# Two heads of an HGRN2 pair make their steps in one job instead of in turn

## The chip, the core and the metric

The kernel runs on one core of a Trainium2 chip. Its time is the device time of one execution in microseconds (us); of the kernel before, three runs gave a median of 1096.72 us (1095.92 to 1097.88). Engines go by the profile's names: PE is TensorE (its weight loads are PEld), DVE is VectorE, ACT is ScalarE, POOL is GpSimd, SP is the engine that issues most DMAs.

## What is computed

Two layers of an encoder over 512 tokens of 1024 channels. Each layer normalises x, multiplies it with one wide matrix, feeds four head groups A, B, C and D, gates each, and adds the product of all four with an output matrix to x. Group A, the part that changes, has four heads of 128 channels; each is a gated linear recurrence, run forwards and backwards over the sequence and added:

```python
def _hgrn2_scan(q, k, v, log_f):
    # S_t = diag(f_t) S_{t-1} + k_t v_t^T, o_t = S_t^T q_t, in chunks
    attn = jnp.einsum('bhtd,bhsd,bhtsd->bhts', qb, kb, decay)
    o = (jnp.einsum('bhts,bhsv->bhtv', attn, vb)
         + jnp.einsum('bhtd,bhdv->bhtv', qb * jnp.exp(b), S))
    ...
# per head: o = rmsnorm(o_forward + o_backward) * silu(z)
```

Group B is windowed attention, C a matrix-memory recurrence, D attention into 256 memory tokens.

## The kernel before

**Projections.** Nearly all of the time is PE work on the projections. Weights come in blocks of 512 KB (`load_w`, line 385); of each block ACT makes a rounded copy `wh` and DVE the rest `wl`, and PE adds three products per tile (`wh` with the high and the low part of the input, `wl` with the high part) into a PSUM tile `pj`. `mm` (line 257) and `gmm` (line 260) issue every product, so nearly all PE rows have L258 or L261; operations on DVE, ACT and POOL all go through one helper and have L152.

**An A head** (`mix_A`, line 550) is a generator that works between these products. It goes through seven levels, block length m = 1, 2, 4 to 64. A level's products are `per_block` (line 566): for m up to 16 sixteen products of 32 weight columns, for m = 32 again 32 columns, for m = 64 eight products of 64 columns, all into one PSUM tile `s`. Level 1 has in addition a first set of 32 products (the diagonal), into a second `s` tile that ACT copies out (line 579). Behind the products of a level DVE multiplies K2 (line 598) and then Q2 (line 601) with the decays of the level, and only then takes the level's products out of PSUM with a predicated copy (line 603, and 608 for m = 32). The pool `ps` (line 223) has two buffers for each name, so there are two `s` tiles at any time. After the levels come transposes of K2 (L635, tile `tr`), the states (`s`), the output (`o`), a root mean square on ACT and DVE (`rsqrt`, line 368, a chain of 12 small DVE operations), and at last the transposes of the normalised output (L669).

**What sets the order.** `Weave` (line 159) keeps the jobs beside the projections. Every group of projection products calls `tick` with its PE time; a job whose due time has come makes its next step there, and is due again after the PE time that it reports plus a latency that it names (`A_LAT0` for the start, `A_LAT` for a level, by pair, `A_LAT2` and `A_LATN` for the tail; in ns, line 73). `join` makes the rest of a job's steps at once. The four heads work as two pairs: pair 0 beside the projections of its own values and of group B, pair 1 beside those of C and D. In a pair the two heads are two jobs, the second set off by half an `A_LAT`, so that they alternate. What is so recorded is then sorted by a scheduler of the framework into one fixed order for each engine; an engine carries out its rows in this order.

Of the kernel before, what the change touches and what calls it, by code (L numbers as in the profile page):

```python
# [14 lines left out]
P = 128  # L15
# [54 lines left out]
              + [O_CK, O_CQ, O_CZ, O_CZ + 256, O_DQ, O_DQ + 256])  # L70
OUT_ORDER = ((0, 1), (2, 3))

A_LAT0, A_LAT, A_LAT2, A_LATN = 5500, (5400, 4600), 500, 27000
B_LATP, B_LAT = 300, 1150
AHEAD = 2
AHEAD_V = 1
# [82 lines left out]
class Weave:  # L159
# [10 lines left out]
    def mark(self, name):  # L170
        self.name = name
        self._mark(name)
# [34 lines left out]
def trunk(tc, a, dbg=None, mark=lambda s: None):  # L207
    wv = Weave(mark)
# [5 lines left out]
    with es:  # L214
# [17 lines left out]
        def u4(shape, dt=F32):  # L232
            return u4p.tile([P] + shape, dt, tag="u4", name=nm("u4"))
# [5 lines left out]
        def a2(shape, dt=F32):  # L239
            return a2p.tile([P] + shape, dt, tag="a2", name=nm("a2"))  # L240
# [144 lines left out]
        def load_w(n, *more):  # L385

            his, los = [], []
            for m in more:
                his.append(m[0])
                los.append(m[1])  # L390
            for _ in range(n - len(more)):
                raw = wp.tile([P, 4, 256], F32, tag="wr", bufs=3, name=nm("wr"))
                hi, lo = [wp.tile([P, 4, 272], F32R, tag=t, bufs=WB, name=nm(t)) for t in ("wh", "wl")]
                sy.dma_start(raw.rearrange("p k c -> p (k c)"), a["wpk"][nblk[0]])
                nblk[0] += 1
                with tc.high_priority() if nblk[0] > 4 else contextlib.nullcontext():
                    act.copy(hi[:, :, 0:256], raw)
                    dve.tensor_tensor(lo[:, :, 0:256], raw, hi[:, :, 0:256].bitcast(F32), ALU.subtract)
                his.append(hi)
                los.append(lo)  # L400
            if n == 1:
                return hi, lo
            return (lambda k: his[k // 4][:, k % 4]), (lambda k: los[k // 4][:, k % 4]), his, los
# [6 lines left out]
        def proj_tok(h, w, n, evac, nt=NC):  # L410

            whi, wlo = w[:2]
            nh = sum(t.ap[1][1] for t in h[0]) // 4
            pts = [pj() for _ in range(nt // 2)]
            for kh in range(nh):
                for c in range(nt):
                    o = pts[c // 2][:, (c % 2) * 256:(c % 2) * 256 + n]
                    for k in range(4 * kh, 4 * kh + 4):
                        hh = rows(h[0], k)[:, c * P:(c + 1) * P]
                        hl = rows(h[1], k)[:, c * P:(c + 1) * P]  # L420
                        last = k == 4 * nh - 1

                        gmm(o, hh, whi(k)[:, :n], k == 0 and c % 2 == 0, False)
                        gmm(o, hh, wlo(k)[:, :n], False, False)
                        gmm(o, hl, whi(k)[:, :n], False, last)
                        if k % 2 == 1:
                            wv.tick(6 * n / 2.4)
                    if kh == nh - 1 and c % 2 == 1:
                        with tc.high_priority():
                            evac(c - 1, pts[c // 2].rearrange("p (c n) -> p c n", c=2)[:, :, :n])  # L430
# [15 lines left out]
        def proj_ch(h, w, evacs, nt=T, bank=pj):  # L446

            whi, wlo = w[:2]
            pts = [bank() for _ in evacs]
            for kh in range(2):  # L450
                for b, pt in enumerate(pts):
                    for k in range(4 * kh, 4 * kh + 4):
                        wh = whi(k)[:, b * P:(b + 1) * P]
                        wl = wlo(k)[:, b * P:(b + 1) * P]
                        hh = rows(h[0], k)[:, 0:nt]
                        hl = rows(h[1], k)[:, 0:nt]
                        mm(pt[:, :nt], wh, hh, start=(k == 0), stop=False)
                        mm(pt[:, :nt], wh, hl, start=False, stop=False)
                        mm(pt[:, :nt], wl, hh, start=False, stop=(k == 7))
                        wv.tick(3 * nt / 2.4)  # L460
                    if kh == 1:
                        with tc.high_priority():
                            evacs[b](pt[:, :nt])
# [54 lines left out]
        def gate_proj(h, w):  # L518
            gz = u4([NC, 256])
            proj_tok(h, w, 256, lambda c0, pv: silu_gate(gz, c0, pv))  # L520
            return gz
# [154 lines left out]
        def group_A(l, h, pr, yT, between=None, before=None, raw=None):  # L676

            mark(f"projA{pr}")
            last_exp.clear()
            if raw is None:  # L680
                w = load_w(2)
                q = [a2([512]) for _ in range(2)]
                proj_ch(h, w, [lambda pv, t=t: act.copy(t, pv) for t in q])
            else:
                q, h0, R, jobR = raw
            F2 = K2 = v = gz = None
            jobs = []

            def ev(pv, b, d):

                with tc.issue_after(last_exp[0].ins) if last_exp else contextlib.nullcontext():
                    act.activation(F2[b][:, d], pv, AF.Sigmoid)
                    act.activation(K2[b][:, 1 - d], pv, AF.Sigmoid, scale=-1.0)
                if l > 0:
                    hd = pr * 2 + b
                    dve.tensor_scalar(F2[b][:, d], F2[b][:, d], oml[:, hd:hd + 1], lb[:, hd:hd + 1], ALU.mult, ALU.add)
                    dve.tensor_scalar(K2[b][:, 1 - d], K2[b][:, 1 - d], oml[:, hd:hd + 1], None, ALU.mult)

            def gates():
                nonlocal F2, K2  # L700
                F2 = [u4([2, 512]) for _ in range(2)]
                K2 = [u4([2, 512]) for _ in range(2)]
                for d in (1, 0):
                    w = load_w(2)
                    if raw is not None:
                        def scaled(pv, b, d):
                            wv.join(jobR)
                            t = a2([512])
                            dve.tensor_tensor(t, pv, R, ALU.mult)
                            ev(t, b, d)  # L710
                        proj_ch(h0, w, [lambda pv, b=b, d=d: scaled(pv, b, d) for b in range(2)], bank=psc if d else pj)
                    else:
                        proj_ch(h, w, [lambda pv, b=b, d=d: ev(pv, b, d) for b in range(2)])

            def values():
                nonlocal v, gz
                w = load_w(2)
                v = u4([NC, 256])
                proj_tok(h, w, 256, lambda c0, pv: act.copy(v[:, c0:c0 + 2], pv))
                if between is not None:  # L720
                    between()
                    mark(f"projA{pr}")
                w = load_w(2)
                gz = gate_proj(h, w)

            def go():
                for b in range(2):
                    jobs.append(wv.spawn(f"mixA{pr * 2 + b}", mix_A(l, pr * 2 + b, F2[b], K2[b], q[b],
                                         lambda c, b=b: v[:, c, b * P:(b + 1) * P],
                                         lambda c, b=b: gz[:, c, b * P:(b + 1) * P], yT), after=b * A_LAT[pr] / 2))  # L730
            if pr == 0:
                gates()
                wv.join(*jobN)
                jobN.clear()
                if raw is not None:
                    jobM.append(wv.spawn("memn", mem_norm(), after=M_LAT))
                go()
                values()
            else:
                values()  # L740
                before()
                mark(f"projA{pr}")
                gates()
                go()
            return jobs
# [454 lines left out]
        def mem_norm():  # L1200
            yield 0, 0
            spread(jobM.pop(0), Rm)
            yield 450, M_LAT2
            mem0.append(mem_kv(0))
            next(mem0[0])
            yield 0, 0
# [284 lines left out]
        for l in range(NL):  # L1491
# [19 lines left out]
            jobs = group_A(l, h, 0, yA, raw=raw)  # L1511
# [3 lines left out]
            b = group_B(l, h)  # L1515
# [10 lines left out]
            jobs = group_A(l, h, 1, yA, lambda: gates.append(next(grC)), lambda: wv.join(jobB, *gates))  # L1526
# [48 lines left out]
```

## Time and profile before

| | |
|---|---|
| median of 3 runs | 1096.72 us |
| profiled execution, its own time | 1095.96 us |
| its span | 1094.2 us |
| PE busy | 1070.1 us, 98% |
| DVE, ACT, POOL busy | 752.9, 545.3, 108.9 us |
| granted TensorE clock, mean | 0.998 of full speed |

The span is what the trace covers, some 1.8 us less than the execution's own time. A busy PE means that a product is under way, not that the array is full. In the rows a line gives the start, the time until the last of the merged instructions ends, engine, source line, operation, tile written and tiles read, shapes and how many instructions were merged; idle time ahead and what ended it stand in brackets. A float32 product that isn't of the rounded type is recorded as two instructions, so the 16 products of a level are 32 records.

### The profile page before, as it was taken

The page shows a single profiled execution, that of the slowest core. Times are in us where ns is not written, and L with a number is a line of the kernel's source. Part 1 is how long each engine was busy: PE and PEld are TensorE (multiplying, and loading weights), DVE is VectorE, ACT ScalarE, POOL GpSimd, SP SyncE. Part 2 cuts the span into 40 slices and gives each one's busy share as a digit, 9 for nine tenths or more (in the row PEclk, how much of TensorE's full clock was granted, in tenths as well). Part 3 has the DMA queues.
Part 4 walks back from the last instruction along what each step waited for, and adds up shares of the span by engine and source line. Part 5 has one row for each costly group of instructions (what it writes and reads, how often), then busy time and mean ns, then how long its engine had stood idle before and what let it go on. Part 6 is the DMA issues. An engine that isn't in the chain of part 4 may idle for free.

```text
span 1094.2 us, 22817 instructions
## 1 busy us (share of the span) xinstructions
PE 1070.1 (98%) x9148; PEld 962.3 (88%) x9148; DVE 752.9 (69%) x1819; ACT 545.3 (50%) x1152; POOL 108.9 (10%) x184
## 2 busy tenths in 40 slices
PE   8999999999999999999999999999999999999997
PEld 6899898998988897887798999889989789889997
DVE  5997547695676958867373776487858668687664
ACT  7645247666435444345473434376754354433544
POOL 0000001220000222011000000013100013020200
PEclk9999999999999999999999999999999999999999
DMA  9332242122223346222443221311122233272111
GB/s 346 104 111 79 74 139 99 40 79 61 81 85 81 106 104 191 74 75 96 152 156 114 79 80 59 95 63 59 61 77 80 78 89 100 95 216 82 59 40 78
DMA packets 36857, 107.62 MB, mean 98 GB/s; under 512 B 6208, under 2 KB 9920, under 8 KB 36752
## 3 DMA queue, kind: packets, MB, share of 16 engines
q1 hardware_dynamic: 36032, 103.67, 29.9%
q0 software_dynamic: 720, 2.50, 0.6%
q8 instruction: 72, 1.18, 0.4%
q14 instruction: 33, 0.27, 0.1%
HBM read 101.89 MB, written 4.26 MB: 97 GB/s over the span
## 4 chain that ended last, share of the span: by engine, by line
PE 78%; DVE 12%; ACT 4%; DMA 3%; issue 1%; POOL 0%; SPq 0%; ACTq 0%; DVEq 0%; POOLq 0%
PE pj L258 34%; PE pj L261 27%; DVE u L152 4%; PE s L258 4%; PE o L258 4%; DVE a L152 3%; PE s L261 3%; DVE wl L152 2%; PE o L261 2%; ACT u L152 1%; PE tr L862 1%; ACT a L152 1%; ACT wh L152 1%; DMA u<-in_memT 1%; DMA u<-in_xT 1%
## 5 line engine op out<-in xcount | busy, mean ns | idle before, releaser
L261 PE MATMUL pj<-wh,u 128*128 128x256 f32 x1984 | 386.7, 286 | 2.8 <-ACT u L152 1.2
L258 PE MATMUL pj<-u,wh 128*128 128x512 f32 (+1 forms) x1216 | 374.8, 389 | 2.5 <-ACT u L152 1.3
L261 PEld LDWEIGHTS pj<-wh,u 128*128 128x128 f32 x1984 | 314.2, 188 | 7.4 <-ACT u L152 1.6
L152 DVE TENSOR_TENSOR wl<-wr,wh 128x1024 fp32r<-128x1024 f32 (+1 forms) x162 | 194.4, 1201 | 123.1 <-ACT wh L152 122.0
L261 PE MATMUL pj<-wl,u 128*128 128x256 f32 x992 | 278.5, 281 | 0.0
L258 PEld LDWEIGHTS pj<-u,wh 128*128 128x128 f32 x1216 | 216.8, 188 | 44.1 <-ACT u L152 2.1
L152 ACT CAST wh<-wr 128x1024 fp32r<-128x1024 f32 (+1 forms) x162 | 164.3, 1015 | 153.5 <-PE pj L258 72.2
L258 PE MATMUL pj<-u,wl 128*128 128x512 f32 (+1 forms) x608 | 232.6, 383 | 0.0
L261 PEld LDWEIGHTS pj<-wl,u 128*128 128x128 f32 x992 | 187.1, 189 | 0.3
L258 PEld LDWEIGHTS pj<-u,wl 128*128 128x128 f32 x608 | 114.2, 188 | 23.0
L152 DVE TENSOR_TENSOR u<-u,a 128x512 f32<-128x512 f32 (+1 forms) x104 | 74.1, 730 | 19.5 <-PE s L261 16.4
L258 PE MATMUL pj<-wh,u 128*128 128x256 f32 (+1 forms) x320 | 62.8, 287 | 0.0
L152 POOL TENSOR_SCALAR u<-u,rB 128x256 f32<-128x256 f32 (+1 forms) x64 | 35.5, 567 | 245.7 <-DVE rB L152 132.1
L258 PEld LDWEIGHTS o<-u,u 128*128 128x128 f32 x384 | 48.2, 191 | 4.5 <-issue 2.5
L258 PE MATMUL o<-u,u 128*128 128x129 f32 (+1 forms) x384 | 50.2, 275 | 1.9 <-DVE dnC L152 1.9
L258 PEld LDWEIGHTS pj<-wh,u 128*128 128x128 f32 x320 | 51.0, 188 | 0.7 <-issue 0.5
L152 POOL TENSOR_TENSOR u<-u,cf 128x512 f32<-128x512 f32 x16 | 22.6, 1412 | 234.4 <-DMA u<-rdr 129.1
L258 PE MATMUL pj<-wl,u 128*128 128x256 f32 (+1 forms) x160 | 45.3, 283 | 0.0
L152 DVE TENSOR_TENSOR u<-u,u 128x512 f32<-128x512 f32 (+2 forms) x48 | 38.7, 838 | 5.7 <-ACT a L152 4.5
L258 PE MATMUL s<-u,a 128*128 128x256 f32 (+1 forms) x224 | 40.6, 301 | 0.0
L152 ACT ACTIVATE u<-u,nmB 128x256 f32<-128x256 f32 (+1 forms) x64 | 35.8, 561 | 8.7 <-DVE nmB L152 6.5
L152 ACT COPY u<-u 128x512 f32<-128x512 f32 x40 | 26.8, 686 | 26.4 <-DVE u L152 13.0
(222 smaller groups left out, 1379.5 us busy)
## 6 DMA issues: line engine op xcount, KB each, us to landing
wr<-in_wpk SPq DMA_DIRECT2D x154, 512.0 KB, 3.5
u<-in_xT SPq DMA_DIRECT2D x16, 256.0 KB, 6.2
u<-rdr SPq DMA_DIRECT2D x16, 256.0 KB, 4.7
u<-gdr SPq DMA_DIRECT2D x16, 192.0 KB, 6.2
u<-in_x SPq DMA_DIRECT2D x4, 512.0 KB
u<-in_memT SPq DMA_DIRECT2D x4, 512.0 KB
xd<-u POOLq DMA_DIRECT2D x4, 512.0 KB, 5.0
u<-xd SPq DMA_DIRECT2D x4, 512.0 KB
```

Source lines behind the costliest of these rows:

```text
L152: r = f(*args, **kw)
L258: nc.tensor.matmul(out, l, r, start=start, stop=stop)
L261: nc.tensor.matmul(out, l, r, start=start, stop=stop, skip_group_check=True)
L862: nc.tensor.transpose(pt[:, j * P:(j + 1) * P], pr[e][:, j * P:(j + 1) * P], ident)
```

## The change

`go` no longer spawns two jobs. It makes both generators, and one job steps them in lock-step: each step of the job issues the step of the first head and then that of the second, reports the sum of their PE times and the longer of their latencies. The latencies in line 73 are longer.

```diff
-A_LAT0, A_LAT, A_LAT2, A_LATN = 5500, (5400, 4600), 500, 27000
+A_LAT0, A_LAT, A_LAT2, A_LATN = 6500, (6600, 5800), 2500, 25000
...
             def go():
-                for b in range(2):
-                    jobs.append(wv.spawn(f"mixA{pr * 2 + b}", mix_A(l, pr * 2 + b, F2[b], K2[b], q[b],
-                                         lambda c, b=b: v[:, c, b * P:(b + 1) * P],
-                                         lambda c, b=b: gz[:, c, b * P:(b + 1) * P], yT), after=b * A_LAT[pr] / 2))
+
+                heads = [mix_A(l, pr * 2 + b, F2[b], K2[b], q[b], lambda c, b=b: v[:, c, b * P:(b + 1) * P],
+                               lambda c, b=b: gz[:, c, b * P:(b + 1) * P], yT) for b in range(2)]
+
+                def both():
+                    for s0, s1 in zip(*heads):
+                        yield s0[0] + s1[0], max(s0[1], s1[1])
+                jobs.append(wv.spawn(f"mixA{pr}", both()))
```

The number of products, copies and DMAs is the same. Outside the four stretches in which a pair works the order of PE stays, but for one set of group C's state products in each layer that moves by some products.

PE at the first level of pair 1 in layer 0. `s_3651` and `s_3686` are the diagonal and the level's products of the first head (`s_3639` and `s_3674` before), `s_3708` and `s_3743` those of the second; `pj` are projection products.

```order
 L261 MATMUL pj_3567<-wh_3561,u_20_113 128x256
+L261 MATMUL s_3651<-a_262_2056,u_548_3420 32x32 x32
+L261 MATMUL s_3686<-u_575_3575,u_576_3577 32x32 x16
 L261 MATMUL s_3708<-a_263_2057,u_549_3421 32x32 x32
-L261 MATMUL s_3743<-u_578_3598,u_579_3600 32x32 x16
 L261 MATMUL pj_3568<-wh_3561,u_15_108 128x256
 L261 MATMUL pj_3568<-wl_3562,u_15_108 128x256
+L261 MATMUL s_3743<-u_578_3580,u_579_3582 32x32 x16
```

The first head's two sets, which stood 12 projection products ahead of the second's, now stand right before them, and the second head's level stands two projection products behind. The other three pairs have the same four rows with the same two products between.

PE at the next level of the same pair: the first head's products (`s_3842`) and the second's (`s_3864`), which had 12 projection products between them.

```order
 L261 MATMUL pj_3805<-wl_3793,u_14_107 128x256
 L261 MATMUL pj_3805<-wh_3792,u_18_111 128x256
+L261 MATMUL s_3842<-u_575_3575,u_546_3418 32x32 x16
+L261 MATMUL s_3864<-u_578_3580,u_547_3419 32x32 x16
 L261 MATMUL pj_3805<-wh_3792,u_13_106 128x256
 L261 MATMUL pj_3805<-wl_3793,u_13_106 128x256
```

The two stand together, with some 60 projection products to the pair before and behind them.

PE at the end of the same pair: the transposes of the first head's output (`tr_4406`) and of the second's (`tr_4415`) among products of 512 columns.

```order
 L258 MATMUL pj_4443<-u_14_107,wl_4424 128x512
-L669 MATMUL tr_4415<-cf,u_547_3419 128x128
+L669 MATMUL tr_4406<-cf,u_546_3418 128x128
 L258 MATMUL pj_4442<-u_15_108,wh_4429 128x512
-L669 MATMUL tr_4415<-cf,u_547_3419 128x128
+L669 MATMUL tr_4406<-cf,u_546_3418 128x128
 L258 MATMUL pj_4442<-u_19_112,wh_4429 128x512
```

Where the second head's transposes stood, the first head's now stand; ahead of them come nine products of the second head's output and seven projection products since the last product of the first head's output. The second head's transposes follow some 24 projection products later.

## Rows read from the trace of the kernel before

**Rows 1.** The page: busy time, and granted clock in tenths by slices.
```profile
PE 1070.1 (98%) x9148; PEld 962.3 (88%) x9148; DVE 752.9 (69%) x1819; ACT 545.3 (50%) x1152; POOL 108.9 (10%) x184
...
PEclk9999999999999999999999999999999999999999
```

**Rows 2.** PE's waits, longest in total first: us in total, times, longest.
```profile
PE o L258 <- DVE dnC L152: 1.9, 2, 1.1
```

**Rows 3.** Windows, two pair stretches: PE, PEld, DVE, ACT, POOL, clock, DMA, GB/s.
```profile
50.00:107.00 57.00, 56.52 (x937) 53.78 (x936) 49.07 (x126) 27.83 (x47) 0.90 (x1) 1.00 0.29 94
286.00:353.00 67.00, 66.88 (x908) 57.30 (x908) 46.91 (x108) 27.99 (x59) 1.29 (x1) 1.00 0.25 75
```

**Rows 4.** PE's timeline around one head's level-4 products.
```profile
306.76 0.41 PE L261 MATMUL pj<-wh,u 128*128 128x256 f32 x2
...
308.19 0.28 PE L261 MATMUL pj<-wh,u 128*128 128x256 f32 x1
308.40 0.46 PE L261 MATMUL s<-u,u 128*32 128x32 f32 x32
308.79 0.38 PE L261 MATMUL pj<-wh,u 128*128 128x256 f32 x1
309.01 0.28 PE L261 MATMUL pj<-wl,u 128*128 128x256 f32 x1
```

**Rows 5.** PE's timeline, first level of pair 1, layer 0, both heads.
```profile
288.51 0.76 PE L261 MATMUL s<-a,u 128*32 128x32 f32 x58
...
289.17 0.54 PE L261 MATMUL s<-u,u 128*32 128x32 f32 x28
289.64 0.39 PE L261 MATMUL pj<-wh,u 128*128 128x256 f32 x1
289.86 0.28 PE L261 MATMUL pj<-wl,u 128*128 128x256 f32 x1
...
291.25 0.82 PE L261 MATMUL s<-a,u 128*32 128x32 f32 x63
...
291.91 0.54 PE L261 MATMUL s<-u,u 128*32 128x32 f32 x31
```

**Rows 6.** ACT's and DVE's timeline, the same place.
```profile
289.40 0.27 ACT L152 COPY a<-s 128x128 f32<-128x128 f32 x1 [1.15 <-PE s L261]
...
288.29 1.23 DVE L152 TENSOR_TENSOR wl<-wr,wh 128x1024 fp32r<-128x1024 f32 x1 [3.53 <-ACT wh L152]
289.43 2.10 DVE L152 TENSOR_TENSOR u<-u,u 128x512 f32<-128x512 f32 x2
291.37 0.32 DVE L152 COPY_PREDICATED a<-cu,s 128x128 f32<-128x128 uint8 x1
```

**Rows 7.** DVE's, then PE's timeline, first level of pair 1, layer 1.
```profile
830.52 0.30 DVE L152 COPY_PREDICATED a<-cu,s 128x128 f32<-128x128 uint8 x1
...
831.05 0.54 PE L261 MATMUL s<-u,u 128*32 128x32 f32 x32
```

**Rows 8.** Output to transposes, pair 1, layer 0: PE, ACT, DVE timelines.
```profile
337.00 2.39 PE L258 MATMUL o<-u,u 128*128 128x128 f32 x20
...
342.42 2.17 PE L258 MATMUL o<-u,u 128*128 128x128 f32 x18
...
350.67 0.39 PE L258 MATMUL pj<-u,wl 128*128 128x512 f32 x1
351.17 0.30 PE L669 MATMUL tr<-cf,u 128*128 128x128 f32 x1
...
339.43 0.28 ACT L152 ACTIVATE u<-o 128x128 f32<-128x128 f32 x1 [2.39 <-PE o L258]
...
340.61 0.17 DVE L152 TENSOR_SCALAR rq_v<-ssA 128x4 f32<-128x4 f32 x1 [3.59 <-ACT u L152]
...
348.50 0.16 DVE L152 TENSOR_SCALAR rq_y<-rq_v 128x4 int32<-128x4 int32 x1
...
350.68 1.13 DVE L152 SCALAR_TENSOR_TENSOR u<-o,rq_y,u 128x128 f32<-128x128 f32 x4
```

**Rows 9.** PE's timeline, a level-16 step of pair 0 in layer 0.
```profile
81.11 0.46 PE L261 MATMUL s<-u,u 128*32 128x32 f32 x32 [0.48 <-DVE rr L152]
```

## The prediction

> **What bounds the kernel now.** I read the page first. PE is busy for 98% of the span, at full clock in every slice [rows 1]: the kernel is as long as PE's queue. The list of PE's waits comes next. Its longest entry is 1.9 us in two waits [rows 2], so little can be won by ending waits, and what PE gains must come from the way its instructions follow each other. The table of stretches confirms it where the change works: while a pair of A heads is under way PE is busy for 56.52 of 57 us and 66.88 of 67 us, at clock 1.00 [rows 3]; the pairs of layer 1 look the same. DVE is busy for 49.07 of 57 us in the first stretch. Then I read PE's timeline at single steps, where a reader can see what inserting a head's step costs.
>
> **Fewer switches on PE.** Look at one head's step among projection products [rows 4]. Twelve products of 256 columns start between 306.76 and 308.19, 0.119 us apart. Around the step, the last one starts at 308.19, the head's 32 records at 308.40, the next projection product at 308.79 and the one after it not before 309.01: 0.82 us for two spacings of 0.119 and the step, which thus costs 0.58. The records themselves take 0.27 of it (0.46 until the last ends, less 0.2 for one record, and one spacing); the rest, 0.31, is paid once for a run of 32-column products, whatever its length. Where two heads' records follow each other, the second costs only its records. In the one place where that is already seen, the 63 diagonal records that run ahead of 31 more, records start 0.66/64 = 0.0103 us apart [rows 5], so 32 more would cost 0.33, and the switch saved would be 0.25. A saved switch is thus worth 0.25 to 0.31; I take 0.29, nearer to the undisturbed step. Runs of 64 columns were not priced apart and are taken alike.
>
> The number of runs follows from PE's order. Before, the four pairs make 57 separate runs of narrow products, and group C's states 4. After, the pairs make 38 (some levels still stand apart, since the scheduler puts a few projection products between the heads), C's states 6. So 61 - 44 = 17 switches go: 17 x 0.29 = **-4.9 us** (4.3 to 5.3). The products of 128 columns in the tail (transposes, states, outputs) I cost at nothing; if each merged tail set saved or lost one projection spacing of 0.12, twelve sets would move 1.4 us, which the range holds.
>
> **A wait that comes in.** Level 1 uses two PSUM tiles for each head, and there are only two `s` buffers. The second head's level-1 products need the buffer that the first head's level-1 products filled, and DVE empties that one only behind the two multiplications. Take the start of the first head's diagonal as zero, 288.51. ACT's copy of the diagonal ends at 289.67, 1.16 later; DVE's multiplications start at 289.43, and the predicated copy ends at 291.69, 3.18 after the start [rows 6]. The other three pairs show 3.2 as well. The weight cast ahead of the multiplications ends as the diagonal does, so it isn't what holds them. How soon PE follows is to be seen in layer 1, where the second head came just too early: copy ended at 830.82, PE started at 831.05 [rows 7], 0.23 later. So the second head's level can start 3.4 after zero. Where would PE be? The first head's sets take 0.99 (the last record starts at 289.17 + 0.54 - 0.21), the second diagonal 0.66, then 0.14 to a projection product, 0.22 to the next and 0.21 back [rows 4, 5]: 2.2 after zero. PE stands still for the difference, 3.4 - 2.2 = 1.2, less some 0.05 that the switch back may overlap: 1.15 in each of four pairs, **+4.6 us**. From below: if PE follows a copy within 0.1, 1.0 each, 4.0; from above: the second diagonal needs ACT's copy, 1.16 and 0.23 after zero, 0.4 past where it would start, and if nothing of that is swallowed by the later wait, 1.4 each, 5.6. Queued behind the waiting products on PE are projection products. DVE and ACT wait for those to take them out of PSUM, but have idle time of their own, and PE has nothing else to do: all of the wait is lost.
>
> The Trainium skill speaks against this change in the same place: "TensorEngine Tiling (Array Packing)", section PSUM Bottleneck, says that tiling speeds up the products but not the emptying of PSUM, which may become the bound. Here the 32-column records take 0.27 us and the emptying 3.2, which agrees; with the rule alone the sum would be the +4.6, with the switches alone -4.9.
>
> **Later levels** need no such wait: the buffer that a level needs was emptied in the level before, some 7 us of products earlier, and DVE's work for both heads of a level is four operations of 0.6 us and two copies. What it hides behind are some 60 projection products. **The tail of pair 1** is tighter than before, since the join leaves little to put between. From the last product of the first head's output to its transposes DVE and ACT need: squares, 339.43 to 340.61, 1.2; the root, 348.50 to 350.68 plus one step, 2.4; the first quarter of the output 0.35; and 0.15 to PE: 4.1. PE has 18 records of the other head, 2.0, and seven products of 512 columns, 1.6 [rows 8]: a wait of 0.45 in two layers, +0.9. The second head's transposes waited 0.27 before (351.17 against 350.67 and 0.23) and now come 7.6 us behind their output: -0.55 for two. Together **+0.35** (-0.5 to 1.5, had the root again to share DVE with other work). **One wait goes**: a level-16 step of pair 0 idled 0.48 us [rows 9]; its successors stand farther apart: **-0.5** (0 to -0.5).
>
> **Sum.** -4.9 + 4.6 + 0.35 - 0.5 = -0.45 us. The profiled execution took 1095.96 us, so 1095.5; the median of the runs is 0.76 above that execution, so **1096.3 us** in its terms. The bounds together give -5.3 + 4.0 - 0.5 - 0.5 = -2.3 and -4.3 + 5.6 + 1.5 = +2.8, or 1094.4 to 1099.5.
>
> **Rivals.** (1) *The wait doesn't bite.* If PE's wait at level 1 is mostly covered, for example because DVE starts its multiplications before the diagonal has ended, only the switches count: 1096.7 - 4.9 + 0.35 - 0.5 = 1091.7 us. For it: the predicated copy itself takes only 0.32. Against it: the multiplications overwrite what the diagonal reads, and the two stand ahead of the copy in DVE's queue [rows 6]. The skill's same page, section Key Properties, says that a change of tiling mode drains the engine; by that rule alone one arrives here. 15%. (2) *DVE becomes the bound, slower.* Both heads' multiplications now stand in a block on DVE, four times 0.6 and two copies of 0.2, 2.8 us, and a weight cast (1.23) that falls behind it is late for PE. Place: pair 0 of layer 0, where DVE is busy for 86% [rows 3]. If six levels each make PE wait 1 us there, 1096.3 + 6 = 1102 us. It decides once a cast ends less than about 2.8 us ahead of its first product. Against it: PE's waits name no cast, and DVE idled 3.53 ahead of one in pair 1 [rows 6]. 12%. (3) *The merge is less than it says*: no, the runs are counted in the order.
>
> **Chances.** A run of this kernel can tell about 0.2%, 2.2 us, from no change. Forecast 73%; it spreads with its bounds mostly within 2.2 us (62 of the 73), 7 below, 4 above. With the rivals: faster 7 + 15 = 22%, same 62%, slower 4 + 12 = 16%. The range goes from 1093.0, part of the way to rival 1, to 1099.5.
>
> **What would show it.** In the profile after: four waits of PE at `s` for DVE, each about 1.1 us, some 2 us after a pair's first diagonal; level steps with 64 records in one run, 0.55 us long; a wait of half a microsecond at the first transposes of pair 1's output; no projection product that waits for a cast. Four waits of well under 1 us, or records spaced wider in the merged runs, would prove the sum wrong on one or the other side.

## The result and the profile after

| | before | after |
|---|---|---|
| median of the runs made together | 1096.80 us (5 runs, 1095.92 to 1098.38) | 1102.07 us (5 runs, 1101.84 to 1105.05) |
| ratio, 95% interval | | 1.0051 (1.0040 to 1.0062) |
| profiled execution, its span | 1094.2 us | 1100.4 us |

The change made the kernel 0.5% slower, where 1096.3 us (1093.0 to 1099.5) was predicted. The page of the kernel after answers to [rows 1], and its list of PE's waits to [rows 2] (engine, tile, line, what it waited for: us in total, times, longest).

```profile
PE 1070.7 (97%) x9148; PEld 963.1 (88%) x9148; DVE 756.3 (69%) x1819; ACT 545.6 (50%) x1152; POOL 110.2 (10%) x184
```

```profile
PE tr L669 <- DVE u L152: 4.3, 4, 1.7
PE s L261 <- DVE a L152: 3.1, 4, 0.8
PE s L261 <- DVE u L152: 2.0, 2, 1.0
...
PE o L258 <- DVE dnC L152: 0.8, 1, 0.8
```

PE is busy for as long as before, and the kernel is 6 us longer: PE waits. The second entry is the predicted one, four times at level 1. The first is new and larger: 4.3 us at the transposes of the heads' output. The two windows of [rows 3] don't hold the same work now, but show the new idle time:

```profile
50.00:107.00 57.00, 56.10 (x918) 54.26 (x918) 45.57 (x119) 25.02 (x39) 0.61 (x1) 1.00 0.29 95
286.00:353.00 67.00, 65.68 (x908) 56.92 (x906) 43.04 (x92) 26.40 (x57) 0.14 (x1) 1.00 0.24 77
```

**Merged levels.** PE's timeline at a level of pair 1, as in [rows 4]: both heads' products stand in one run of 64 records.

```profile
301.42 0.28 PE L261 MATMUL pj<-wh,u 128*128 128x256 f32 x1
301.63 0.78 PE L261 MATMUL s<-u,u 128*32 128x32 f32 x64
302.34 0.38 PE L261 MATMUL pj<-wh,u 128*128 128x256 f32 x1
302.56 0.28 PE L261 MATMUL pj<-wl,u 128*128 128x256 f32 x1
```

From 301.42 to 302.56 is 1.14 us; without two spacings of 0.119 the run cost 0.90. Two separate runs of 0.58 [rows 4] cost 1.16, so a merge saves 0.26.

**Level 1.** PE, then ACT and DVE, first level of pair 1, layer 0 [rows 5, 6].

```profile
290.83 0.76 PE L261 MATMUL s<-a,u 128*32 128x32 f32 x58
...
291.49 0.54 PE L261 MATMUL s<-u,u 128*32 128x32 f32 x28
292.04 0.86 PE L261 MATMUL s<-a,u 128*32 128x32 f32 x64
292.83 0.39 PE L261 MATMUL pj<-wh,u 128*128 128x256 f32 x1
293.06 0.28 PE L261 MATMUL pj<-wl,u 128*128 128x256 f32 x1
294.11 0.54 PE L261 MATMUL s<-u,u 128*32 128x32 f32 x32 [0.78 <-DVE a L152]
```

```profile
291.73 0.27 ACT L152 COPY a<-s 128x128 f32<-128x128 f32 x1 [0.19 <-PE s L261]
...
291.73 2.10 DVE L152 TENSOR_TENSOR u<-u,u 128x512 f32<-128x512 f32 x2 [1.31 <-PE s L261]
293.67 0.29 DVE L152 COPY_PREDICATED a<-cu,s 128x128 f32<-128x128 uint8 x1
```

The second head's products start at 294.11, 3.28 behind the first diagonal, where 3.4 was predicted, and 0.15 behind the end of DVE's copy (293.96), where I took 0.23 [rows 7]. From the projection product at 293.06 to them is 1.05 us where an undisturbed switch takes 0.21: the wait costs 0.84. The second diagonal starts late as well: the last product ahead of it started at 291.82 (291.49 and 0.54, less 0.21 for one record), and it comes at 292.04, as soon as ACT has copied the first (292.00). Together that is 1.05 us in a pair, 4.2 in four.

**Tail of pair 1, layer 0.** PE first [rows 8], then DVE, then POOL.

```profile
345.90 4.18 PE L258 MATMUL o<-u,u 128*128 128x128 f32 x36
...
352.17 0.30 PE L669 MATMUL tr<-cf,u 128*128 128x128 f32 x1 [0.46 <-DVE u L152]
...
357.49 0.62 PE L258 MATMUL pj<-u,wh 128*128 128x512 f32 x2
359.75 0.30 PE L669 MATMUL tr<-cf,u 128*128 128x128 f32 x1 [1.64 <-DVE u L152]
```

```profile
352.71 0.16 DVE L152 TENSOR_SCALAR rq_v<-ssA 128x4 f32<-128x4 f32 x1
352.78 1.22 DVE L152 TENSOR_TENSOR wl<-wr,wh 128x1024 fp32r<-128x1024 f32 x1
353.92 1.26 DVE L152 TENSOR_SCALAR rq_y<-rq_v 128x4 int32<-128x4 int32 x1
355.09 0.74 DVE L152 SCALAR_TENSOR_TENSOR u<-tr,par,u 128x512 fp32r<-128x512 f32 x1
...
357.12 1.15 DVE L152 TENSOR_TENSOR rq_t<-rq_y 128x4 f32<-128x4 f32 x1
...
358.59 0.75 DVE L152 SCALAR_TENSOR_TENSOR a<-a,par,a 128x512 f32<-128x512 f32 x1
359.25 1.12 DVE L152 SCALAR_TENSOR_TENSOR u<-o,rq_y,u 128x128 f32<-128x128 f32 x4
```

```profile
352.86 2.29 POOL L152 TENSOR_TENSOR u<-u,cf 128x512 f32<-128x512 f32 x1 [91.69 <-DMA u<-rdr]
356.93 1.32 POOL L152 TENSOR_TENSOR u<-u,cf 128x512 f32<-128x512 f32 x1 [1.77 <-DMA u<-rdr]
```

The second head's output ends at 350.08, but DVE begins its root at 352.71, behind the first head's root and output. Into this chain fall a weight cast, two long steps of other jobs, and two steps of 128x4 that last 1.26 and 1.15 us instead of 0.16. Both lie under POOL's two mask additions for group C. PE comes at 357.95 (357.49 and two spacings of 0.23), and waits until 359.75. Layer 1 shows the same picture: waits of 0.47 and 1.75 us, and two 128x4 steps of 1.29 and 1.24 us.

```profile
901.78 0.30 PE L669 MATMUL tr<-cf,u 128*128 128x128 f32 x1 [1.75 <-DVE u L152]
```

In before the second root had ended at 350.7, just ahead of POOL's additions. POOL, then DVE, layer 0 of before:

```profile
351.68 1.29 POOL L152 TENSOR_TENSOR u<-u,cf 128x512 f32<-128x512 f32 x1 [91.39 <-DMA u<-rdr]
351.94 2.11 DVE L152 TENSOR_TENSOR wl<-wr,wh 128x1024 fp32r<-128x1024 f32 x1
```

There POOL came first, and it was DVE's weight cast that took 2.11 us instead of 1.22.

**Where the time went.** For each kernel I took the start of the same PE product ahead of and behind a stretch. The table gives what the stretch takes more than in before, in us, from one profiled run of each kernel (the start counts from the span's start); the columns behind "after" are experiments told below.

| stretch (before's time) | after | longer latencies | old latencies | early pair 1 | split |
|---|---|---|---|---|---|
| start, to 39.9 | +1.5 | +1.2 | +1.0 | +0.6 | +0.9 |
| pair 0, layer 0, 39.9 to 162.7 | -0.8 | -1.0 | +0.1 | -0.4 | -2.2 |
| pair 1, layer 0, 286.6 to 367.6 | +2.3 | +2.8 | +1.7 | +0.3 | -0.6 |
| C's states, 379.0 to 385.8 | +0.7 | +0.8 | 0.0 | 0.0 | 0.0 |
| C's last products, 416.5 to 441.7 | -0.7 | -0.1 | +1.4 | +1.4 | +1.4 |
| pair 0, layer 1, 613.2 to 729.5 | +0.8 | +0.7 | +1.0 | +1.1 | -0.7 |
| pair 1, layer 1, 825.7 to 905.9 | +2.0 | +2.1 | +1.4 | -0.9 | -1.8 |
| C's states, 918.4 to 925.2 | +0.7 | +0.8 | 0.0 | 0.0 | 0.0 |
| whole span | +6.2 | +7.6 | +6.2 | +1.5 | -3.4 |

The start holds the same instructions in the same order everywhere; its difference is none of the change's, and the last section returns to it and to the row of C's last products. Pair 1 is the place: +4.3 us in two layers.

### The profile page after: what moved, and what is told of

Read it like the earlier page. It is cut to its first block, busy times and chain, and to the rows that moved or that the text cites. A ratio compares the mean times of both kernels' runs of the same rounds, so it can differ in the third digit from the quotient of the medians.

```text
span 1100.4 us, 22823 instructions
## 1 busy us (share of the span) xinstructions
PE 1070.7 (97%) x9148; PEld 963.1 (88%) x9148; DVE 756.3 (69%) x1819; ACT 545.6 (50%) x1152; POOL 110.2 (10%) x184
## 4 chain that ended last, share of the span: by engine, by line
PE 77%; DVE 12%; ACT 5%; issue 2%; DMA 2%; POOL 1%; SPq 0%; ACTq 0%; POOLq 0%; DVEq 0%
PE pj L258 33%; PE pj L261 27%; PE o L258 5%; PE s L258 5%; DVE u L152 4%; DVE a L152 3%; PE s L261 2%; DVE wl L152 2%; ACT u L152 2%; ACT a L152 2%; ACT wh L152 1%; PE o L261 1%; PE tr L866 1%; DMA u<-rdr 1%; DVE rq_t L152 1%
## 5 line engine op out<-in xcount | busy, mean ns | idle before, releaser
L261 PE MATMUL pj<-wh,u 128*128 128x256 f32 x1984 | 379.8, 285 | 2.4 <-ACT u L152 1.2
L152 ACT ACTIVATE u<-o,dnC 128x128 f32<-128x128 f32 x32 | 11.7, 367 | 55.3 <-DVE dnC L152 54.0
```

What stands on the lines that cost most here:

```text
L152: r = f(*args, **kw)
L261: nc.tensor.matmul(out, l, r, start=start, stop=stop, skip_group_check=True)
```

## The experiments

My theory after the result had three parts: the wait at level 1; lateness (the longer latencies, and steps that report both heads' PE time, move pair 1's tail up against the join, where DVE has other work and is held by POOL); and merges that do save what they should. The rivals: lock-step itself puts one root behind the other; DVE is what bounds; switches cost nothing.

**1. Longer latencies alone**, heads alternating as before.

```diff
-A_LAT0, A_LAT, A_LAT2, A_LATN = 5500, (5400, 4600), 500, 27000
+A_LAT0, A_LAT, A_LAT2, A_LATN = 6500, (6600, 5800), 2500, 25000
```

> The kernel before with the four longer latencies alone; the two heads of a pair still alternate in two jobs. Lateness theory (the longer latencies move pair 1's tail up against the join, where DVE also has a weight cast to make and is held by POOL, so that PE waits for both heads' output there): PE waits about 0.6 us at the first head's output transposes and 1.5 to 2 us at the second's in each layer, none of the switches is saved and the level-1 bank wait does not come: 1096.8 + 4 = about 1101 us. Rival (it is the lock-step itself that puts the second head's root behind the first head's on DVE): no wait above 0.5 us at these transposes, 1096 to 1098 us.

1104.08 us against 1097.08 of before, ratio 1.0067 (1.0052 to 1.0082): at least as slow as the whole change, and 3 us above what I expected, which left out C's states (1.6 us in two layers) and the start (1.2). PE's timeline in the tails of pair 1, layer 0 and layer 1:

```profile
349.61 0.30 PE L669 MATMUL tr<-cf,u 128*128 128x128 f32 x1 [0.46 <-DVE u L152]
...
354.63 0.30 PE L669 MATMUL tr<-cf,u 128*128 128x128 f32 x1 [0.68 <-DVE u L152]
356.90 0.59 PE L669 MATMUL tr<-cf,u 128*128 128x128 f32 x2 [0.57 <-DVE u L152]
...
898.49 0.30 PE L669 MATMUL tr<-cf,u 128*128 128x128 f32 x1 [1.82 <-DVE u L152]
```

The waits at the transposes come without any lock-step, and C's states lose 0.8 us in each layer, as in after (0.7). Lock-step isn't needed for either; lateness is enough.

**2. Lock-step alone**, with the latencies of before.

```diff
-A_LAT0, A_LAT, A_LAT2, A_LATN = 6500, (6600, 5800), 2500, 25000
+A_LAT0, A_LAT, A_LAT2, A_LATN = 5500, (5400, 4600), 500, 27000
```

> The changed kernel (lock-step) with the four latencies of before. Lateness theory: the four waits at level 1 stay (4 x 1.07); pair 1's output products come 11 rows of PE (some 2.5 us) earlier than in the changed kernel, but still behind those of before, so PE still waits at the output transposes, 0.3 to 0.6 us for the first head and 0.5 to 1.5 us for the second, and C's states stay split: 1099 to 1101 us. Rival (the longer latencies alone did the harm, and lock-step with the old ones gives what was hoped): no wait at these transposes, 1096 to 1097.5 us.

1103.19 us, ratio 1.0053 (1.0040 to 1.0066), 2 us over the expected range; of the time over before, 1.4 us stand in C's last products and 1.0 in the start (last section). The first head's transposes waited 0.45 us in layer 0, the second's 0.65 and 0.53, and in layer 1 1.58. C's states did not split, against what I expected: that belongs to the longer latencies alone. So the old latencies don't help. With both heads' PE time in each step, pair 1 is late all the same: its output begins at 343.04, where before had the first head's at 337.00 [rows 8] and after both at 345.90.

**3. POOL's two additions left out.** This kernel leaves out the masks of group C's first head in each layer, and with them a part of the computation.

```diff
-                        gp.tensor_tensor(own, own, V(mge ...
+                        if hd > 0:
+                          gp.tensor_tensor(own, own, V(mge ...
```

> The changed kernel; POOL's two mask additions for the first head of group C are left out in each layer (part of the computation is missing). Theory (in pair 1's tail two of these POOL instructions hold DVE for 1.1 us each in the middle of the second head's root chain, and that makes PE wait 1.8 us at its transposes): DVE's 128x4 steps there take 0.16 us each, the wait at the second head's transposes is under 0.2 us in both layers, 1102.1 - 3.6 = about 1098.5 us. Rival (the weight cast and the other DVE work in the chain alone hold it, POOL's records only lie beside it): wait still over 1 us, 1101 to 1102.5 us.

1100.24 us over 12 runs, ratio 1.0024 (1.0012 to 1.0036): 1.8 us less than after, half of what was expected in the time. In the trace pair 1 takes 1.7 and 1.5 us less than in after, near the expected 1.8 each. The second head's chain on DVE, then PE:

```profile
355.00 0.16 DVE L152 TENSOR_SCALAR rq_y<-rq_v 128x4 int32<-128x4 int32 x1
...
357.44 0.16 DVE L152 TENSOR_TENSOR rq_t<-rq_y 128x4 f32<-128x4 f32 x1
```

```profile
359.14 0.30 PE L669 MATMUL tr<-cf,u 128*128 128x128 f32 x1
```

With cast, evacuation and the long step still in the chain, the 128x4 steps are back at 0.16, and PE's wait of 1.64 is gone (0.29 is left of layer 1's 1.75). Without POOL's hold the chain is in time; what the cast and the other steps add was not taken out, so their shares aren't shown. The median's smaller gain is in part the clock: the three runs with a mean granted clock of 0.998 or more took 1097.3 to 1099.0 us and the three of after with 0.998 took 1101.8 to 1102.1, but the other nine of the twelve here had 0.997 or less. The profiled run is the slowest of the twelve: from 975 to 985 us and in C's last products its clock was 0.83, where after's was 1.00 (last section). How much of the missing 1.8 us that explains isn't shown.

**4. Another bank for the second diagonal.**

```diff
-            def per_block(n, qv, *ks):
-                p = psc()[:, :NC * n].rearrange("p (c q) -> p c q", c=NC)
+            def per_block(n, qv, *ks, bank=psc):
+                p = bank()[:, :NC * n].rearrange("p (c q) -> p c q", c=NC)
...
+                           bank=po if hd % 2 else psc)
```

> The changed kernel, with the second head's diagonal in a PSUM tile of the name o instead of s, so that the second head's level 1 takes the buffer that ACT's copy of the first diagonal frees. Theory (the two-buffer wait at level 1 costs 1.07 us in each of four pairs): the four waits of PE at s for DVE go, one extra early single diagonal product adds 0.3 us in two places at most: 1102.1 - 4.3 + 0.5 = about 1098.3 us. Rival (PE would wait as long for something else there, e.g. K2 and Q2 of the level, or DVE is what bounds): 1101 to 1103 us.

1101.92 us, ratio 1.0043 (1.0027 to 1.0058): the theory's 1098.3 did not come. Yet the four waits are gone, and the stretches of the pairs are 0.8, 0.2, 0.9 and 0.9 us shorter than in after. The edit does more than move a bank: with no wait between them, both heads' diagonals and level 1 now stand in one run of 192 records, one run fewer in each pair (34 in place of 38), and in all pairs but pair 1 of layer 0 PE waits some 0.3 us at `pj` for ACT a little later. The two are about equal, so some 0.9 us is what the level-1 wait was worth in those three. The odd one is pair 1 of layer 0, PE's timeline:

```profile
294.19 0.39 PE L261 MATMUL pj<-wh,u 128*128 128x256 f32 x2
295.53 0.28 PE L261 MATMUL pj<-wl,u 128*128 128x256 f32 x1 [0.95 <-issue]
```

PE stood 0.95 us for nothing that the profile shows, a little behind the run of 192. The other losses are in C's last products, 416.5 to 441.7, 2.6 us more than in after, and in the start, 0.7 more. In experiment 6 the same edit gives all that was expected.

**5. Pair 1 early**, lock-step kept.

```diff
-A_LAT0, A_LAT, A_LAT2, A_LATN = 6500, (6600, 5800), 2500, 25000
+A_LAT0, A_LAT, A_LAT2, A_LATN = 6500, (6600, 3400), 500, 25000
```

> The changed kernel (lock-step) with pair 1's level latency 3400 instead of 5800 ns and the tail's 500 instead of 2500: pair 1's output products then stand some 40 rows of PE earlier, well ahead of the join. Lateness theory: no PE wait at either head's output transposes (0.6 and 1.8 us in each layer before), the level-1 bank wait stays: 1102.1 - 4.9 - 0.6 (one merged 64-column run more per layer) = about 1096.6 us; with C's states back in their old place up to 1.3 less. Rival (lock-step itself needs the longer latencies, DVE makes both heads' multiplications and casts and PE waits at the levels instead): new waits at s of 0.5 to 1 us at several levels, 1100 to 1103 us.

1097.24 us, ratio 0.9997 (0.9988 to 1.0006): 4.8 us less than after, where 5.5 was expected and C's states in their old place besides. Pair 1 takes 2.0 and 2.9 us less and C's states 0.7 less in each layer, but C's last products 2.1 more. The levels show no new waits. PE's timeline in layer 0 has output and transposes of both heads in one run each, 10 us apart, without a wait:

```profile
334.83 4.63 PE L258 MATMUL o<-u,u 128*128 128x128 f32 x40
...
344.86 1.36 PE L669 MATMUL tr<-cf,u 128*128 128x128 f32 x8
```

The same early place for the heads that alternate (before, with `(5400, 3400)`):

> The kernel before (alternating) with pair 1's level latency 3400 instead of 4600. Theory (the early place of pair 1 only takes away what the longer latencies brought, and before had none of it): the tail waits of before, 0.27 for the second head in each layer, go, nothing else changes: 1096 to 1097 us. Rival (the early place is worth as much for alternating heads, and merging gives nothing): under 1095 us. If DVE cannot follow at 3400: waits at s, over 1098 us.

1098.20 us, ratio 1.0009 (0.9999 to 1.0018), 1 us above the expected range. Early brought nothing where there was no lateness: the second head's transposes wait no longer, but PE now waits 0.41 and 0.44 us at level 1 of pair 1 for DVE, waits that before's list does not have.

**6. Early, and the other bank** (edits 4 and 5 together).

> Lock-step, pair 1's latency 3400 and the tail's 500 (as the run with the early pair 1), and the second head's diagonal in an o tile (as the run with the other bank). If the terms add: 1097.2 - 4.3 + 0.3 = about 1093.2 us. Rival (the time that the bank wait takes is filled by something else, as the run with the other bank gained less than the four waits): 1095 to 1097 us.

1093.12 us, ratio 0.9964 (0.9949 to 0.9978). The terms add: 4.1 us below experiment 5, of which the four runs fewer (32 in place of 36) are some 1 us.

**7. Early, and the diagonals in a step of their own.** Both heads' diagonals go in one run and both level 1 in the next, so that the level's two `s` tiles take the buffers that ACT's copies freed.

```diff
             act.copy(ac, pd)
+            yield 560, 1500
             Tm = F2
```

> Lock-step with the early pair 1, and a step of its own for the diagonals: both heads' diagonals in one run, 1500 ns later both heads' level 1 in one run, so that both level-1 tiles take s buffers that ACT has long emptied. Theory: no wait of PE at s for DVE at level 1, the number of runs of narrow products falls to 8 for each pair: 1097.2 - 4.3 - 0.6 = about 1092.3 us. Rival (levels and tail 1.5 us later bring waits elsewhere): 1095 to 1098 us.

1092.56 us, ratio 0.9952 (0.9939 to 0.9964): the fastest kernel, 0.5% below before. Pair 1 has as many narrow runs here as in experiment 5, eight in each layer, and takes 0.9 and 1.0 us less: that is the wait at level 1 alone. PE's timeline, pair 1 of layer 0:

```profile
288.64 1.48 PE L261 MATMUL s<-a,u 128*32 128x32 f32 x128
...
292.37 0.87 PE L261 MATMUL s<-u,u 128*32 128x32 f32 x58
293.47 0.28 PE L261 MATMUL s<-u,u 128*32 128x32 f32 x6 [0.23 <-issue]
293.68 0.39 PE L261 MATMUL pj<-wh,u 128*128 128x256 f32 x1
```

None of these rows waits for DVE.

**8. The same, unmerged:** the second head's step comes one tick behind the first's.

```diff
-                    for s0, s1 in zip(*heads):
-                        yield s0[0] + s1[0], max(s0[1], s1[1])
+                    for s0 in heads[0]:
+                        yield s0[0], 0
+                        s1 = next(heads[1])
+                        yield s1[0], max(0, max(s0[1], s1[1]) - 1500)
```

> As the run with the diagonals in a step of their own (1092.6 us), but the second head's step comes one tick behind the first head's, so that six projection products stand between them: 64 runs of narrow products instead of 32, nothing else made later. Theory (a switch between projection and narrow products costs PE 0.25 to 0.31 us wherever it stands): 1092.6 + 32 x 0.28 = about 1101.5 us, with no new waits. Rival (what the run with the split gained came from the waits it removed, switches cost nothing by themselves): 1092 to 1095 us.

1100.20 us, ratio 1.0029 (1.0016 to 1.0042). Against experiment 7 that is 7.6 us for 32 runs more, 0.24 each; by the four stretches of the pairs it is 8.5 us, 0.26 each, with 0.5 us of small new waits in it. PE's timeline of one level:

```profile
297.00 0.46 PE L261 MATMUL s<-u,u 128*32 128x32 f32 x32
...
298.29 0.46 PE L261 MATMUL s<-u,u 128*32 128x32 f32 x32
```

The rival that switches are free fell.

**9. Pair 0 early as well** (`5500, (5200, 3400)`, over experiment 7).

> As the run with the diagonals in a step of their own, with pair 0 earlier too (start 5500, level latency 5200 instead of 6500 and 6600). Theory (what pair 0 still loses in layer 1, some 0.7 us in small waits beside group B's transposes, comes from its late tail, as in pair 1): 1091.5 to 1092 us. Rival (pair 0's DVE, busy for 86%, cannot follow at 5200): waits at s, 1093 to 1096 us.

1095.38 us over 9 runs (1092.47 to 1097.44), ratio 0.9984 (0.9973 to 0.9994): 2.8 us slower than experiment 7 in the median, in the rival's range. The profiled run, the fastest of the nine, has the span of experiment 7, 1090.7 against 1090.8 us; pair 0 takes 0.2 us more in layer 0 and 0.6 more in layer 1, and PE has no wait at the levels for DVE. So the rival's mechanism isn't shown either, and where the slower runs lose isn't known; being earlier did not help pair 0.

## Why the prediction was wrong

**The step that failed is the tail's**: "The second head's transposes waited 0.27 before [...] and now come 7.6 us behind their output: -0.55 for two." I counted the distance on PE and took DVE's chain at its length alone, as if it started with the output. It starts behind the first head's chain, at 352.71 instead of some 351.3 (the output's end and 1.2 for the squares), and a cast, two steps of other jobs and two holds by POOL, some 1 us each, fall into it. So although PE did come 7.9 us behind the output (357.95 less 350.08), it waited 1.64 and 1.75 us. Against the two waits of 0.27 before, that is +2.85 where -0.55 stood, 3.4 us off. I even gave an upper bound for a root that shares DVE, but only +1.5, and did not ask what else DVE and POOL begin at the join.

The Trainium skill has the rule that was missing: "SBUF — State Buffer", section Who interferes with whom, says that DVE and GpSimd share a pair of ports, that a tensor_scalar in its fast mode or an operation with two SBUF inputs may need it, and, of the fast mode, that whoever issues first keeps it for the whole instruction. The rows agree on both sides: DVE's 128x4 steps lasted 1.26 and 1.15 under POOL's additions, and POOL's first addition lasted 2.29 against 1.32 for its second, beside DVE's cast of 1.22. Experiment 3 has the 0.16 without them.

**The first head's wait** was right: 0.45 predicted, 0.46 and 0.47 measured, 0.9 in all.

**The switches** were right. Predicted 0.29 each (0.25 to 0.31); 0.26 at a single level and 0.24 over 32 runs in experiment 8, so the 17 gave some 4.1 to 4.4 us instead of 4.9. The Trainium skill's sentence on draining at a change of tiling mode ("TensorEngine Tiling (Array Packing)", section Key Properties) fits in that a switch costs something; it names no price, and no run here shows the drain itself.

**The wait at level 1** was right in mechanism, place and time, +4.6 predicted. The rows give 1.05 in the pair shown, 4.2 us in four. Taking it away gave 0.9 and 1.0 in pair 1 in experiment 7, where the number of runs stays, and 0.8 to 0.9 in three pairs in experiment 4. The rival that the wait doesn't bite fell.

**C's split states** were counted as two switches of 0.29. They cost 0.7 us in each layer, and they too came from the longer latencies.

**The level-16 wait** of 0.48 [rows 9] did go in the profile of after. In the run without POOL's additions, whose order is the same there, one of 0.65 came back near 86 us, and with the old latencies one of 0.89. That term is not settled.

**Pair 0** of layer 1 was 0.8 us longer, where five runs fewer and the level-1 wait make -0.2. A new wait of PE at `pj` for ACT, 0.29 at 726.13, is a part of it. Lateness there too would explain the rest: the longer latencies alone give +0.7, but pair 0 earlier gave nothing over experiment 7. This stays open.

The sum by measured prices: -4.75 (19 runs fewer in the pairs at 0.25; C's two more are in its 1.4) + 4.2 + 3.4 + 0.9 - 0.55 (the waits of before at the second head) + 1.4 - 0.5 = +4.1, beside 5.3 between the medians; pair 0 of layer 1 is some 1 us of the difference. The rival "DVE becomes the bound" named 1102 us, but in pair 0's levels and through late casts. No product of PE waited for a cast there; the number was right by chance.

## What to carry to other kernels

Distance on the critical engine is cover only if the chain that runs beside it really starts where you think: for each chain, write down what stands ahead of it on every engine it passes, at its new place, other jobs' work included. A change that delays a job must be priced at the job's end, where a join makes all that is left at once. And when a change both saves and costs, the saving is not lost: with the place and the bank mended, the same merge made this kernel 0.5% faster.

## What was unexpected in the hardware

**TensorE's clock.** The same instructions took different times, for the most part where the granted clock fell (windows: us, then busy time and count of PE, PEld, DVE, ACT, POOL, then clock, DMA share, GB/s). The start, in before and after:

```profile
5.00:15.00 10.00, 7.46 (x33) 5.73 (x32) 8.26 (x23) 8.39 (x17) 0.00 (x0) 1.00 1.04 377
```

```profile
5.00:15.00 10.00, 8.33 (x30) 6.53 (x29) 8.09 (x23) 7.99 (x16) 0.00 (x0) 0.83 1.03 366
```

And 430 to 440 us, in after and in the kernel with the other bank:

```profile
430.00:440.00 10.00, 8.49 (x49) 6.87 (x47) 8.55 (x20) 5.78 (x15) 4.09 (x4) 1.00 0.82 273
```

```profile
430.00:440.00 10.00, 7.57 (x34) 5.96 (x33) 8.72 (x23) 4.96 (x12) 3.67 (x3) 0.85 0.82 269
```

Part of each second window ran at 1.2 GHz. The clock is not the whole of the start's difference: early pair 1 and split kept 1.00 in that window, and PE waited 0.61 and 1.10 us for DVE near 24 us instead. At 430 us PE waits for the end of group C, for 1.38 and 1.05 us in the kernel with the other bank, and the clock fell behind that. Before has two waits there too and kept 1.00, so the waits alone don't decide it. The six experiments with 0.83 to 0.85 from 430 to 440 us (the other bank, old latencies, no POOL additions, early, early with the other bank, split) took 1.0 to 1.9 us more for C's last products than before. After and the four with 1.00 (longer latencies, unmerged, alternating and early, pair 0 early) took between 0.7 less and 0.1 more. So a fall of the clock costs here some 1.5 us, and I found no edit that goes with it; stretches are therefore a better witness than single spans.

**PE without a releaser.** A little behind the long runs of narrow products in pair 1 of layer 0, PE stood 0.95 us (experiment 4), 0.97 in experiment 6, and 0.23 us in the middle of a run in experiment 7, each time put down to "issue". Experiment 1, whose heads alternate, has 0.20 us at the same place. The other three pairs of these runs showed none. What holds PE there is open.
